# Attention in steps, output products two steps behind, projections spread between score pieces

## The chip, the cores and the metric

The kernel runs on one core of a Trainium2 chip. The metric is the device time in microseconds (us), lower is better. The median of three runs of the kernel before is 2564.09 us, with 2552.84 and 2574.48 as the lowest and highest.

The engines of a core each run their own instruction list in order: TensorE (PE, matmuls; PEld are its weight loads), VectorE (DVE), ScalarE (ACT), GpSimd (POOL) and SyncE (SP, which here mostly issues DMAs). An instruction that waits holds back everything behind it on its engine.

## What is computed

One layer of a streaming encoder: 2048 positions, width 1024, with eight heads of banded attention (a query sees its own 64-frame chunk and eight chunks before it) and four heads of differential attention (each made of two softmax maps over all earlier chunks, the second subtracted with a factor), then an output projection and a gated feed-forward part with a short convolution. Cut to what matters:

```python
h = rmsnorm(x, attn_norm_g[l])
qa, ka, va, qb, kb, vb = jnp.split(h @ w_in[l], 6, axis=-1)
...
# band heads: scores over 9 chunks of 64 keys + relative bias, softmax, times v
# differential heads, per block of 128 queries:
sc = jnp.einsum("bqhd,bkhd->bhqk", qblk, k) * (HEAD_DIM ** -0.5)
sc = jnp.where(allowed, sc + bias, -jnp.inf)
p = jax.nn.softmax(sc, axis=-1).reshape(b, B_HEADS, 2, Q_BLOCK, s)
w = p[:, :, 0] - lam * p[:, :, 1]
o = jnp.einsum("bhqk,bkhe->bqhe", w, v)
...
x = x + jnp.concatenate([oa, ob], axis=-1) @ w_out[l]
u = causal_dwconv(rmsnorm(x, ffn_norm_g[l]) @ w_up[l], conv_w[l], conv_b[l])
gate, val = jnp.split(u, 2, axis=-1)
x = x + (jax.nn.silu(gate) * val) @ w_down[l]
return rmsnorm(x, final_norm_g)
```

## The kernel before

**Numbers.** Every large product is done in float16 with each float32 factor split into a high and a low part; three of the four part products are summed (`TERMS`). So a projection of 512 positions takes 8 x 3 = 24 matmuls of 512 columns, and a block of probabilities times values takes three matmuls.

**Slots.** Attention runs in eight slots, `ORDER = [4, 5, 0, 6, 1, 7, 2, 3]`. Numbers 4 to 7 are the differential heads (long rows: tile i of 128 queries sees 128(i+1) keys, so up to 2048); here they are called B slots, and they are the slots 0, 1, 3 and 5. Numbers 0 to 3 are pairs of band heads (at most 640 keys); these are the A slots 2, 4, 6 and 7. Each slot has 16 tiles of 128 queries, in order, in four groups of four.

**One tile.** Scores go to PSUM for both maps of a piece of up to 512 keys (L426 and L428: the high and the low part of q, into tiles `s`). VectorE adds the bias, takes the running maximum and moves the piece to SBUF in one instruction (L474 in A, L524 in B; `St`). After the last piece ScalarE takes the exponential (L481, L530), in B VectorE combines the two maps (L546), ScalarE and GpSimd split the result into float16 parts `phl` (L482 and L483; L548 and L549), SP issues a DMA that transposes it into `pt` (L484, L551), and TensorE multiplies `pt` with the values into `o` (L495, L557). VectorE takes `o` out (`osb`, L497, L559). Scores, exponential, transpose and output products of one tile are one step of a generator (`attn_a`, `attn_b`).

**Projections.** Beside a slot's attention, the kernel projects what is needed next: q of the following group of 512 positions (`proj_q`, tiles `qs`), and after each group of four tiles k and v of the same positions for the next slot's head (`proj_k`, `proj_v`). Their matmuls are L372, with weights `whl` that `load_w` reads, scales and splits for all three of q, k and v at the start of the slot before. ScalarE and VectorE take each result out of PSUM (`split`, L127 and L128). With two small DMAs for each `qs` tile (L416, L417), issued on ScalarE's queue, q is copied to the other half of the partitions.

**The end of attention.** The output projection (`out_proj`, L625, 768 matmuls of 512 columns, tiles `omm`) is done in two parts. Whole quarters of the first part are put between the tiles of the last slot by the table `LAST`; its weights are loaded and split (`load_wo`) at that slot's start. Then come the feed-forward part's up projection (L762) and down projection (L1161).

**What sets the order.** No order is written out by hand: a scheduler places each instruction in its engine's list, by the order of the code and by priorities. Attention steps run under `high_priority(offset=HA)`, the PSUM evictions of the projections under `HP`; the projection matmuls have no such offset. Buffers that bear on the order: three PSUM banks for projections, four for scores, one for the four small `o` tiles; eight granules of `St`, two `phl`, three `pt`, eight each of `ks` and `vs`, two `qs`, four `whl`, two raw weights.

## Time and profile before

| | us or share |
|---|---|
| median of three runs | 2564.09 (2552.84 to 2574.48) |
| the profiled execution's own time | 2562.97 |
| its span | 2560.9 |
| TensorE busy | 2389.8 (93%) |
| VectorE busy | 1894.7 (74%) |
| ScalarE busy | 1401.5 (55%) |
| GpSimd busy | 1171.0 (46%) |
| mean granted TensorE clock | 0.956 |

Busy time counts instructions that do work. TensorE's matmuls overlap and their ends are modelled, so 100% busy says that something was always under way. The granted clock is TensorE's, as a share of full speed; at a lower clock the same matmuls fill more busy time. A window of the trace gives these figures for a stretch of time, so that stages can be told apart. A wait names the instruction that waited and what released it.

### The profile page before, as it was taken

The numbers are of one execution on the slowest core, as the hardware profiler recorded it, in microseconds if no ns is written. First come the engines' busy times: TensorE is split into PE (matmuls) and PEld (weight loads), VectorE is DVE, ScalarE is ACT, GpSimd is POOL, SyncE is SP. The second block draws the span as 40 slices with busy tenths as digits, with TensorE's granted clock in tenths as the row PEclk, the third lists the DMA queues.
The fourth block names the chain that finished last, engine by engine and source line by source line (L and its number), as shares of the span: only waits on it lengthen the run. The fifth ranks groups of instructions, "written<-read, shape, count | busy, mean of one in ns | idle before, by whom it ended". The sixth has DMA issues, their size and how long they took to land.

```text
span 2560.9 us, 39466 instructions
## 1 busy us (share of the span) xinstructions
PE 2389.8 (93%) x13878; PEld 1146.9 (45%) x13878; DVE 1894.7 (74%) x4391; ACT 1401.5 (55%) x2431; POOL 1171.0 (46%) x1127
## 2 busy tenths in 40 slices
PE   5799998989897999989869999999999999999998
PEld 4544444544454444444434444444444444444443
DVE  6669786877876797757665888888887886656545
ACT  5547556755675567655434656665656564323322
POOL 2315334332433252123343566656665664756654
PEclk8898998989898989989989999999999999999999
DMA  7224545863677359989978333333323329323322
GB/s 211 57 54 88 104 78 103 143 128 73 112 134 137 58 105 200 191 177 255 278 203 207 123 110 116 100 128 104 122 95 126 104 92 404 121 89 110 112 87 78
DMA packets 631222, 340.48 MB, mean 133 GB/s; under 512 B 448920, under 2 KB 597712, under 8 KB 629616
## 3 DMA queue, kind: packets, MB, share of 16 engines
q1 hardware_dynamic: 615264, 316.15, 48.7%
q10 hardware_dynamic: 12592, 10.26, 1.5%
q0 software_dynamic: 3168, 11.56, 1.4%
q8 instruction: 108, 1.77, 0.3%
q14 instruction: 90, 0.74, 0.1%
HBM read 148.87 MB, written 85.21 MB: 91 GB/s over the span
## 4 chain that ended last, share of the span: by engine, by line
PE 53%; DMA 8%; DVE 8%; issue 4%; ACT 4%; POOL 2%; SPq 2%; ACTq 0%; DVEq 0%; POOLq 0%
PE mm L762 27%; PE mm L1161 13%; PE mm L372 7%; DMA pt<-phl 5%; PE omm L625 2%; PE s L428 2%; DMA wd<-gd 2%; PE s L426 1%; SPq L996 1%; PE o L557 1%; DVE St L524 1%; ACT St L481 1%; ACT phl L482 1%; DVE hl L649 1%; DVE St L546 1%
## 5 line engine op out<-in xcount | busy, mean ns | idle before, releaser
L762 PE MATMUL mm<-T,wuhl 128*128 128x512 f16 x3696 | 802.8, 380 | 24.8 <-ACT tmp L933 22.4
L762 PEld LDWEIGHTS <-wuhl 128*128 128x128 f16 x3696 | 361.9, 98 | 457.8 <-issue 25.9
L372 PE MATMUL mm<-h,whl 128*128 128x512 f16 x2208 | 535.1, 389 | 0.1
L1161 PE MATMUL mm<-wd,ghl 128*128 128x512 f16 x1848 | 401.8, 380 | 2.9 <-ACT ghl L127 1.8
L372 PEld LDWEIGHTS <-whl 128*128 128x128 f16 x2208 | 205.7, 100 | 250.1 <-issue 38.2
L549 POOL TENSOR_TENSOR phl<-St,phl 128x1024 f16<-128x1024 f32 (+4 forms) x96 | 155.7, 1632 | 304.2 <-ACT phl L548 292.6
L1161 PEld LDWEIGHTS <-ghl 128*128 128x128 f16 x1848 | 180.7, 98 | 223.4 <-ACT ghl L127 2.9
L961 DVE SCALAR_TENSOR_TENSOR Y<-U,taps,Y 128x1024 f32<-128x1024 f32 x176 | 257.3, 1462 | 3.9 <-ACT Y L957 2.4
L530 ACT ACTIVATE St<-St,nb,sc 128x1024 f32<-128x1024 f32 (+4 forms) x192 | 188.1, 981 | 88.3 <-DVE nb L527 87.5
L426 PE MATMUL s<-ks,qs 128*128 128x128 f16 (+3 forms) x720 | 196.1, 303 | 41.7 <-DVE mxb L524 32.7
L127 ACT ACTIVATE ghl<-wd,gsc 128x384 f16<-128x384 f32 (+1 forms) x176 | 106.6, 659 | 195.6 <-DMA wd<-gd 89.7
L128 DVE SCALAR_TENSOR_TENSOR ghl<-wd,gsc,ghl 128x384 f16<-128x384 f32 (+1 forms) x176 | 136.9, 812 | 95.1 <-ACT ghl L127 94.4
L524 DVE CUSTOM_DVE_ANT_0 St<-s,near,mxb 128x512 f32<-128x512 f32 (+3 forms) x280 | 168.7, 624 | 40.6 <-PE s L428 34.7
L483 POOL TENSOR_TENSOR phl<-St,phl 128x640 f16<-128x640 f32 (+2 forms) x64 | 82.4, 1287 | 243.8 <-ACT phl L482 198.7
L428 PE MATMUL s<-ks,qs 64*128 64x128 f16 (+3 forms) x720 | 182.8, 307 | 0.0
L625 PE MATMUL omm<-wohl,oT 128*128 128x512 f16 x672 | 159.2, 391 | 8.7 <-DVE x L629 8.6
L871 POOL TENSOR_TENSOR Sx<-wuraw 128x512 f32<-128x512 f32 x44 | 77.8, 1769 | 171.5 <-ACT wuraw L862 153.9
L965 ACT ACTIVATE Y<-Y 128x1024 f32<-128x1024 f32 x44 | 46.5, 1057 | 179.7 <-DVE Y L961 179.7
L557 PE MATMUL o<-vs,pt 128*128 128x128 f16 x1632 | 123.9, 231 | 21.0 <-DMA pt<-phl 16.4
L792 DVE SCALAR_TENSOR_TENSOR wdhl<-wdraw,wd_sc,wdhl 128x128 f16<-128x128 f32 x132 | 134.6, 1038 | 11.6 <-ACT wdhl L789 10.9
L428 PEld LDWEIGHTS <-qs 64*128 64x128 f16 x720 | 54.4, 93 | 180.9 <-issue 165.2
L481 ACT ACTIVATE St<-St,nb,sc 128x640 f32<-128x640 f32 (+4 forms) x128 | 107.9, 844 | 39.8 <-DVE nb L478 36.7
(227 smaller groups left out, 3868.6 us busy)
## 6 DMA issues: line engine op xcount, KB each, us to landing
wd<-gd SPq DMA_DIRECT2D x88, 256.0 KB, 2.8
wuraw<-in_w_up_dram SPq DMA_DIRECT2D x42, 512.0 KB, 5.0
gd<-Y SPq DMA_DIRECT2D x42, 512.0 KB, 5.3
wdraw<-in_w_down_dram SPq DMA_DIRECT2D x154, 128.0 KB, 2.8
wd<-wdd SPq DMA_DIRECT2D x11, 1792.0 KB, 12.0
wdd<-wdhl SPq DMA_DIRECT2D x41, 448.0 KB, 2.6
wraw<-in_w_in_dram SPq DMA_DIRECT2D x24, 512.0 KB, 4.3
td<-hl SPq DMA_DIRECT2D x24, 512.0 KB, 4.0
```

The lines of the kernel that those rows point to most:

```text
L128: V.scalar_tensor_tensor(lo, src, scale, hi, ALU.mult, ALU.subtract)
L372: nc.tensor.matmul(ps, lhsT=hl[:, a, c, :], rhs=h[:, b, c, :], start=n == 0, stop=n == 3 * NC - 1)
L426: nc.tensor.matmul(ps[hd], lhsT=qs[:, hd, 0, qc], rhs=ks[:, hd, kc], start=True, stop=False)
L428: nc.tensor.matmul(ps[hd], lhsT=qs[a:b, hd, 1, qc], rhs=ks[a:b, hd, kc], start=False, stop=True)
L524: V.tensor_tensor_reduce(Sm[hd][g][:, a0:a0 + b - a], ps[hd][:, :b - a], bias, 1.0, m[hd], ALU.add, ALU.max, mx[:, hd, f:f + 1])
L530: A.activation(Sm[hd][g], Sm[hd][g], AF.Exp, bias=nb[:, hd:hd + 1], scale=w["sc"], accum_out=l[:, hd, g:g + 1])
L549: nc.gpsimd.tensor_tensor(hl[:, 1], Sm[0][g], hl[:, 0], ALU.subtract)
L557: nc.tensor.matmul(o, lhsT=pt[:, a_, j], rhs=vs[:, c_, kt % 4, :], start=kt == 0 and k_ == 0, stop=kt == i and k_ == 2)
L625: nc.tensor.matmul(ps[n], lhsT=oc[:, a], rhs=wo[ORDER[c]][:, b, n * TG:(n + 1) * TG], start=k == 0, stop=k == 3 * NC - 1)
L762: nc.tensor.matmul(ps, lhsT=hl[:, a, wop, c * P:(c + 1) * P], rhs=Tt[:, b, c, :], start=start and k == 0, stop=k == 11, skip_group_check=n ...
L961: V.scalar_tensor_tensor(Y, self.U[j][:, tap:D + tap], self.u.taps[j][:, tap:tap + 1], Y, ALU.mult, ALU.add)
L1161: nc.tensor.matmul(ps[m].rearrange("p (c n) -> p c n", c=4), lhsT=g[kb][:, a, go], rhs=wd[kb][:, :, c_, wo_], start=kb == k0 and k == 0, s ...
```

## The change

The change rewrites the attention stage's order of work; the feed-forward part and every formula stay.

1. Each tile is cut in two: `front_a`/`front_b` (scores to `pt`) and `back_a`/`back_b` (output products). The back part of a tile is written `LAG = 2` steps after its front.
2. The B slots no longer take the tiles 0 to 15 in order but 0, 15, 1, 14, 2, 13 and so on, a short row beside a long one. Steps run on over slot boundaries.
3. Projections are generators that yield after every 6 matmuls (12 of q). `units(n)` lists what a slot has to project, and each step takes its share (48 chunks over 16 steps; 32 in slot 6, 28 over 11 steps in slot 7), divided over the tile's score pieces.
4. q is projected in halves of 256 positions (tiles `mq` and `qs`, four smaller `qs` buffers), since the tiles are no longer taken in groups of four. That makes 64 such projections of 24 matmuls of 256 columns in place of 32 of 512.
5. The three weights of the next head are scanned and loaded at different steps (`beside`), k of the head after next already at steps 13 and 14. In slot 6 the scans for later stages, and in slot 7 `load_wo`, also have steps of their own.
6. The last slot keeps part of its own k and v projections (groups 2 and 3) as fill; the output projection's first part starts at its step 11, in pulls of four chunks of 6 matmuls.
7. One buffer of `x1k` and the call of `make_profiles` move.

The diff, cut to its core:

```diff
+NH2 = 8
+LAG = 2
...
+        def project(ps, hl, h, t0, t1, step):
             n = 0
             for c in range(NC):
                 for a, b in TERMS:
+                    nc.tensor.matmul(ps, lhsT=hl[:, a, c, :], rhs=h[:, b, c, t0:t1], start=n == 0, stop=n == 3 * NC - 1)
                     n += 1
+                    if n % step == 0 and n < 3 * NC:
+                        yield
...
-            qs = kv.tile([P, 2, 2, TG], F16, name="qs", bufs=2)
-            ps = project(w, tg, 0)
+            ps = ps_mm.tile([P, 2 * P], F32, name="mq", tag="mm")
+            yield from project(ps, w["hl"][0], hT[i0 // 4], i0 % 4 * P, (i0 % 4 + 2) * P, 12)
+            qs = w["q"][w["halves"][k]] = kv.tile([P, 2, 2, 2 * P], F16, name="qs", bufs=4)
...
+        def front_b(w, i):
...
+            for f, (a, b) in enumerate(reversed(pieces(0, W, (F,)))):
+                ps = [ps_s.tile([P, 512], F32, name="s") for hd in range(2)]
+                scores([p_[:, :b - a] for p_ in ps], w, i, a, b)
...
                 yield
...
+        def back_b(w, i):
+            pts, rl = w["P"].pop(i)
...
+            for pt, kt0, n in pts:
+                for j in range(n):
...
+                    if j % 4 == 3 and kt < i:
+                        yield
...
-                    xt = kv.tile([P, D], F32, name="x1k", tag="qs", bufs=2) if pc and sd else \
+                    xt = sb.tile([P, D], F32, name="x1k", tag="HL", bufs=2) if pc and sd else \
...
+                                if k % 6 == 0 and k < 3 * NC:
+                                    yield
...
+            order = list(range(NT)) if p < 4 else [i for a in range(NT // 2) for i in (a, NT - 1 - a)]
...
+        def units(n):
+            w = ws[n]
+            q = [proj_q(w, k) for k in range(2, 8)]
+            if n == NH2 - 1:
+                kv_ = [[proj_k(w, g), proj_v(w, g)] for g in (2, 3)]
+                return q[:2] + kv_[0] + q[2:4] + kv_[1] + q[4:]
+            x = ws[n + 1]
+            k, v = [proj_k(x, g) for g in range(NG)], [proj_v(x, g) for g in range(NG)]
+            qx = [proj_q(x, 0), proj_q(x, 1)]
+            if n == NH2 - 2:
+                return q[:2] + [k[0]] + q[2:4] + [k[1], v[0]] + q[4:] + [v[1]] + qx
+            return q[:2] + k[:2] + q[2:4] + k[2:] + q[4:] + v[:2] + qx + v[2:]
...
+        CHUNKS = {NH2 - 2: 32, NH2 - 1: 28}
+        UNTIL = {NH2 - 1: 11}
...
+                    want = CHUNKS.get(n, 48) * (s_ + 1) // steps - got if s_ < steps else 0
+                    got += want
+                    for k in range(slots):
+                        with tc.high_priority(offset=HA):
+                            next(fr)
...
+                        with tc.high_priority(offset=HA):
+                            pull(back, 2)
+                        pull(fill, want * (k + 1) // slots - want * k // slots)
...
+                    if n == NH2 - 1 and s_ >= steps:
+                        pull([first], 4)
```

How this moves TensorE's list is seen at two places. The first is the long row of tile 14 in slot 5 (head 7). Here `qs_...` is its q, `ks_...` its k, `s_...` the score tiles; `mm_...` is a projection for the next slot with weights `whl_...`. Before, pieces of scores follow one another:

```order
L426 LDWEIGHTS qs_10270
L426 MATMUL s_11032<-ks_9134,qs_10270 128x512
L428 LDWEIGHTS qs_10270
L428 MATMUL s_11032<-ks_9134,qs_10270 128x512
L426 LDWEIGHTS qs_10270
L426 MATMUL s_11033<-ks_9134,qs_10270 128x512
L428 LDWEIGHTS qs_10270
L428 MATMUL s_11033<-ks_9134,qs_10270 128x512
L426 LDWEIGHTS qs_10270
L426 MATMUL s_11040<-ks_8767,qs_10270 128x512
L428 LDWEIGHTS qs_10270
L428 MATMUL s_11040<-ks_8767,qs_10270 128x512
```

In the change, TensorE has at the same tile:

```order
L376 MATMUL mm_10462<-h_568,whl_9896 128x512
L376 LDWEIGHTS whl_9896
L376 MATMUL mm_10462<-h_568,whl_9896 128x512
L438 LDWEIGHTS qs_9948
L438 MATMUL s_10577<-ks_8926,qs_9948 128x512
L440 LDWEIGHTS qs_9948
L440 MATMUL s_10577<-ks_8926,qs_9948 128x512
L376 LDWEIGHTS whl_9896
L376 MATMUL mm_10462<-h_568,whl_9896 128x512
L376 LDWEIGHTS whl_9896
L376 MATMUL mm_10462<-h_568,whl_9896 128x512
L376 LDWEIGHTS whl_9896
```

Projection matmuls of 512 columns now stand before and behind a single piece of scores, where before three pieces' matmuls stand in a row.

The second place is the boundary from slot 4 (A) to slot 5 (B), where the output products of slot 4's last tile are placed (L495 before, L515 after; `pt_...` is a tile's transposed probabilities, `vs_...` its values). Before, the products of the next slot's tiles 0 (`pt_9690`) and 1 (`pt_9721`) follow it directly:

```order
L495 MATMUL o_117<-vs_8082,pt_9431 128x64
L495 LDWEIGHTS pt_9431
L495 MATMUL o_117<-vs_8082,pt_9431 128x64
L557 LDWEIGHTS pt_9690
L557 MATMUL o_117<-vs_8430,pt_9690 128x128
L557 LDWEIGHTS pt_9690
L557 MATMUL o_117<-vs_8430,pt_9690 128x128
L557 LDWEIGHTS pt_9690
L557 MATMUL o_117<-vs_8430,pt_9690 128x128
L557 LDWEIGHTS pt_9721
L557 MATMUL o_117<-vs_8430,pt_9721 128x128
L557 LDWEIGHTS pt_9721
```

In the change, the products of slot 4's last tile (`pt_10097`) stand behind scores of the next slot's first long row (not shown) and a projection of q (`mq_...`, 256 columns):

```order
L376 MATMUL mq_10260<-h_1094,whl_9262 128x256
L376 LDWEIGHTS whl_9262
L376 MATMUL mq_10260<-h_1094,whl_9262 128x256
L376 LDWEIGHTS whl_9262
L376 MATMUL mq_10260<-h_1094,whl_9262 128x256
L515 LDWEIGHTS pt_10097
L515 MATMUL o_117<-vs_8425,pt_10097 128x64
L515 LDWEIGHTS pt_10097
L515 MATMUL o_117<-vs_8425,pt_10097 128x64
L515 LDWEIGHTS pt_10097
L515 MATMUL o_117<-vs_8425,pt_10097 128x64
L515 LDWEIGHTS pt_10097
```

The next slot's own output products (L557 before, L589 after) come only after some 20 more projection matmuls and further scores.

## Rows read from the trace of the kernel before

**Rows 1.** Windows by stage: stretch, length, busy per engine, PEclk, DMA share, GB/s

```profile
core 0: us, PE busy (x) PEld busy (x) DVE busy (x) ACT busy (x) POOL busy (x), PEclk, DMA share, GB/s
...
95.00:263.00 168.00, 151.30 (x900) 70.42 (x897) 126.00 (x396) 93.86 (x183) 63.49 (x36) 0.91 0.38 74
263.00:432.00 169.00, 153.03 (x963) 76.00 (x962) 131.56 (x401) 97.50 (x194) 60.34 (x36) 0.89 0.48 92
432.00:520.00 88.00, 88.00 (x715) 44.61 (x714) 65.49 (x211) 61.65 (x122) 22.87 (x16) 0.97 0.76 135
520.00:698.00 178.00, 159.89 (x1064) 78.85 (x1062) 142.52 (x417) 101.03 (x198) 69.27 (x40) 0.88 0.51 98
698.00:786.00 88.00, 87.94 (x729) 45.34 (x726) 70.04 (x217) 66.25 (x131) 24.04 (x17) 1.00 0.77 144
786.00:959.00 173.00, 150.59 (x1025) 72.35 (x1025) 136.97 (x412) 98.34 (x194) 65.26 (x38) 0.90 0.48 95
959.00:1053.00 94.00, 89.59 (x732) 45.70 (x729) 70.57 (x222) 67.50 (x134) 25.87 (x18) 1.00 0.90 187
1053.00:1315.00 262.00, 240.86 (x1630) 116.44 (x1627) 178.18 (x410) 141.23 (x227) 82.89 (x61) 0.94 0.91 227
1315.00:2561.00 1246.00, 1205.62 (x5593) 547.61 (x5591) 905.93 (x1425) 620.02 (x961) 729.35 (x842) 0.99 0.40 130
```

**Rows 2.** Windows, same columns: the eight gaps of the four long-row slots

```profile
790.00:820.00 30.00, 13.54 (x171) 8.64 (x168) 23.54 (x77) 14.99 (x37) 15.42 (x11) 0.72 0.84 157
920.00:950.00 30.00, 24.05 (x129) 10.11 (x129) 27.68 (x86) 22.37 (x39) 19.86 (x10) 0.72 0.43 96
sum 200.00, PE 134.56 PEld 67.34 DVE 166.73 ACT 116.86 POOL 121.81; mean PE 16.82 PEld 8.42 DVE 20.84 ACT 14.61 POOL 15.23
```

**Rows 3.** Windows, same columns: the stretch between two of these gaps

```profile
828.00:922.00 94.00, 94.00 (x567) 43.17 (x564) 74.57 (x235) 53.86 (x106) 21.81 (x15) 1.00 0.36 69
```

**Rows 4.** Waits of TensorE, 95 to 1053 us: waiting line, releaser, total, times, longest

```profile
PE s L426 <- DVE mxb L524: 32.7, 24, 4.7
PE o L557 <- DMA pt<-phl: 16.4, 5, 8.1
```

**Rows 5.** Waits of TensorE, 1053 to 1315 us

```profile
PE omm L625 <- DVE x L629: 8.6, 3, 6.2
```

**Rows 6.** Timeline of TensorE at two gaps: start, us, instruction [idle before <-releaser]

```profile
815.12 0.82 PE L557 MATMUL o<-vs,pt 128*128 128x128 f16 x6 [8.10 <-DMA pt<-phl]
...
930.87 0.58 PE L426 MATMUL s<-ks,qs 128*128 128x512 f16 x1 [4.73 <-DVE mxb L524]
```

**Rows 7.** Chain of waits, pieces in order of time: start, us, what

```profile
894.08 1.51 PE o L557 x27
...
1423.20 36.28 PE mm L762 x168
```

**Rows 8.** Costliest groups of the page: weight loads of the projections

```profile
L372 PEld LDWEIGHTS <-whl 128*128 128x128 f16 x2208 | 205.7, 100 | 250.1 <-issue 38.2
```

**Rows 9.** Tile qs: count, duration ns min/median/max, first and last start, form

```profile
L127 ACT ACTIVATE qs<-mm x64: 571/592/592, 54.4 to 1104.1; 64x512 f16<-64x512 f32 x64
L128 DVE SCALAR_TENSOR_TENSOR qs<-mm,qs x64: 658/689/695, 56.4 to 1107.0; 64x512 f16<-64x512 f32 x64
L416 ACTq DMA_DIRECT2D qs<-qs x32: 468/468/557, 55.0 to 1101.1; - x32
```

**Rows 10.** Groups by shape, 95 to 1053 us: busy, mean, idle before

```profile
L530 ACT ACTIVATE St<-St,nb,sc 128x1024 f32<-128x1024 f32 x80 | 98.5, 1231 | 57.0 <-DVE nb L527 56.9
...
L546 DVE SCALAR_TENSOR_TENSOR St<-St,ratio 128x1024 f32<-128x1024 f32 x36 | 58.1, 1615 | 0.7
...
L549 POOL TENSOR_TENSOR phl<-St,phl 128x1024 f16<-128x1024 f32 x40 | 87.2, 2183 | 118.4 <-ACT phl L548 110.5 <-issue 7.7
```

**Rows 11.** The transposes of L551: issue ns min/median/max, and landing

```profile
L551 SPq DMA_TRANSPOSE pt<-phl x96: 1168/1648/3821, 101.3 to 982.9; - x96
...
DMA to landing us min/median/max: 2.3/4.2/7.2
```

More of the change, by code (lines that the diff above doesn't have):

```diff
@@ L652, in out_proj, with weights, run @@
                         hl.rearrange("p n a d -> p n (a d)"))
[L653 to L660 removed]
+        def weights(n):
+            p = ORDER[n]
+            order = list(range(NT)) if p < 4 else [i for a in range(NT // 2) for i in (a, NT - 1 - a)]
+            halves = []
+            for i in order:
+                if i // 2 not in halves:
+                    halves.append(i // 2)
+            return dict(p=p, order=order, halves=halves, hl={}, E={}, raw={}, k={}, v={}, q={}, P={}, o={}, ssq={})
+        def run(unit):
+            for _ in unit:
+                pass
+        w = weights(0)
         xts, raws = [], []
@@ L724 @@
-        for _ in out_proj(1):
-            pass
+        run(proj_q(w, 1))
+        make_profiles()
+        ws = [w] + [weights(n) for n in range(1, NH2)]
+        first = out_proj(0)
+        def units(n):
[10 more added lines that the diff above has]
+            return q[:2] + k[:2] + q[2:4] + k[2:] + q[4:] + v[:2] + qx + v[2:]
@@ L728, in down_scale @@
+        attention()
     def down_scale(k1):
```

409 lines of the change are left out of this document (217 added, 192 removed).

## Prediction

> **What bounds the kernel now.** I read the windows by stage first, and there only two columns: TensorE's busy time against the length, and its granted clock. From 1315 us on (feed-forward) TensorE is busy 1205.62 of 1246 us at clock 0.99; the change doesn't touch this half. The three A slots from 432 to 1053 us are the same picture: 88.00 of 88, 87.94 of 88, 89.59 of 94. The four B slots are not: 151.30 of 168, 153.03 of 169, 159.89 of 178 and 150.59 of 173, at clocks of 0.88 to 0.91 [rows 1]. Together they take 688 us, of which TensorE is busy 614.8 and idle 73.2.
>
> Second, windows within the B slots. TensorE's idle time is not spread evenly. Between 828 and 922 us it is busy 94.00 of 94 at clock 1.00 [rows 3], while eight stretches (110 to 130, 230 to 250, 370 to 400, 410 to 430, 530 to 550, 650 to 680, 790 to 820, 920 to 950 us; 200 us in all) hold 200 - 134.56 = 65.4 us of the 73.2. Two of them stand in the rows: TensorE busy 13.54 and 24.05 of 30, clock 0.72 in both [rows 2]. So idle time and low clock come at the same places: a slot's beginning, where the first rows are short, and its last long rows.
>
> Third, the waits. Up to 1053 us TensorE waits mostly for two things: 32.7 us for VectorE to free a score bank and 16.4 us for transposed probabilities [rows 4]. The timeline puts one of each at the two places of the order that are shown with the change: at 815.12 the products of a short row waited 8.10 us for their transpose, with nothing else in the list; at 930.87 a long row's scores waited 4.73 us for VectorE [rows 6]. In both, projections had run out. In the rows between, VectorE works 74.57 of 94 us and is not waited for at all [rows 3]. The B slots thus lose time since the filling is in the wrong places, not because there is too much work for one engine.
>
> **What the B slots' work is worth.** The lost clock is 168 x 0.09 + 169 x 0.11 + 178 x 0.12 + 173 x 0.10 = 72.4 us of full speed [rows 1]. What of it fell into idle time costs nothing: between 72.4 x 0.67 = 49 us (busy as in the gaps, 134.56 of 200) and 72.4 x 0.89 = 65 us (busy as in the whole slots) was lost while busy. The low clock is mostly in the gaps, so I take 50. TensorE's work at full clock is then 614.8 - 50 = 565 us, and 688 - 565 = 123 us is friction. VectorE's work there is 126.00 + 131.56 + 142.52 + 136.97 = 537 us [rows 1], close behind.
>
> **The change, part by part.**
>
> Spreading the projections and alternating short and long rows. A matmul of 512 columns takes 36.28 / 168 = 216 ns at full clock, one of an output product 1.51 / 27 = 56 ns [rows 7]. With these prices I counted the order. Before, the projections beside the eight pairs of steps of slot 3 are worth 2.2, 10.4, 11.4, 13.2, 9.1, 12.3, 5.8 and 9.7 us; after, 8.1, 10.3, 9.8, 9.7, 11.3, 7.0, 9.9 and 5.7. The empty first pair is filled, and the other B slots look alike (slot 5's first pair: 1.3 before, 7.1 after). Over the four B slots projections fall from 290 to 283 us; 7 us move to the last slot. That leaves 558 us of work. The friction lies between nothing left (558) and all 123 left (681). I take 52 left, 610 us or 152 a slot. I don't go lower, for VectorE's share rises to some 90% (below), and the nearest row for that load is the gap at 920, where VectorE is busy 27.68 of 30 and TensorE only 24.05 [rows 2]; I don't go higher, for the loads of a pair of steps after the change are now alike (in slots 3 and 5 TensorE has 15 to 21 us per pair, VectorE 11 to 19), and where filling was there nothing waited [rows 3]. **B slots: 610 - 688 = -78.**
>
> Output products two steps behind. They add no work. Counted in the order, between a long tile's last scores and its first output product TensorE has 20 to 26 us of other work (before: 19 to 30). The chain to be hidden, for two maps of two granules: four exponentials of 1.23, the combination of 1.62, a copy no longer than an exponential, GpSimd's 2.18, an issue of up to 3.82 and a landing of 4.2, together 18 us [rows 10, 11]. It fits, and before, with the same cover, all the long rows gave at most 8 us of waiting (16.4 in five places, 8.10 of it at the short row) [rows 4, 6]. A buffer of `pt` is read out 12 us or more before its third successor's first product at nearly every tile (before: from 7), against 8 for issue and landing. I price it at nothing; if the cover falls short, this is the second rival.
>
> q in halves. 1536 matmuls of 256 columns in place of 768 of 512. Between the 56 ns for 128 columns and 216 for 512 lies 109 ns, so +1.6 us, which is inside the counts above. The evictions go from 64 to 128 on each of ScalarE and VectorE; one of 512 columns takes 0.592 and 0.689 us [rows 9]. The extra lies between 0 (half size, half time) and 64 x 0.689 = 44 us of VectorE; I take 20, ten of them in the B slots: 547 of 610 us, 90%. 64 more DMA issues of 0.468 us on ScalarE's queue [rows 9] are 30 us over eight slots; ScalarE is busy 93.86 to 101.03 us per B slot [rows 1], so the slack covers them.
>
> Weight loads. At each of these matmuls new weights are loaded: 768 more loads of 100 ns each [rows 8]. Output products also load new weights for each, and 27 of them took 1.51 us, less than 27 loads one after the other [rows 7, 8]. I price the loads at nothing.
> The Trainium skill ("TensorE: Matmul & The Clock Gate", Part 3, "What overlaps and what doesn't") says that a weight load overlaps with matmuls under way only when their row groups differ; by it the added loads, all of one row group, would cost 77 us. The row of 27 products contradicts that here.
>
> A slots. TensorE has 265.5 us of work in 270 [rows 1], less 2.6 by the counts. The steps now run over slot boundaries, so B's last long rows reach into them. From 263 (nothing waits) to 284 (8% of friction as in B after); I take 276. **+6.**
>
> Last slot and output projection. Before, TensorE is busy 240.86 of 262 [rows 1]. Projections moved in: 80 matmuls of 512 before, 96 of 512 and 100 of 256 after, 16 x 0.216 + 100 x 0.109 = +14 us. Of the output projection, 278 of 768 matmuls stood before the last scores, now 84: 42 us of TensorE work move behind the attention. If the 21 idle us swallow all, 255 (-7); if the attention is held by VectorE at its old length, +42. Near the middle, **+20**, since VectorE (178.18 of 262) and its waits (8.6 us for `x`) [rows 1, 5] don't hold TensorE for long.
>
> Sum: -78 + 6 + 20 = -52. The profiled execution took 2562.97, so 2511; the median of the runs, 2564.09, is 1.1 above it, which I leave out.
>
> **The rivals.**
>
> *VectorE becomes the bound of the B slots.* Its 547 us run in an in-order list with waits for scores, copies and outputs; if it keeps only 85% busy, B takes 643 us: -45 + 26 = -19, **2544**. For it: it works 83% even over the eight gaps (166.73 of 200) [rows 2]. Against: 92% in the gap at 920.
>
> *Slower: the output products run into their transposes.* Each B slot has eight long rows, 32 in all. A wait of 1.6 us at each eats the 52 us, 2.4 us each makes it slower by 1%. The chain of 18 us would have to become 28 against the 25 of the cover, by POOL, SP and ScalarE serving the short row in between; then 3 us x 32 = 96, **2607**. For it: SP issues in order, and landings reach 7.2 us [rows 11]. Against: the cover before was no longer, and the waits few.
>
> *The added weight loads are not hidden*: 2511 + 77 = **2588**. The row of 27 products speaks against it.
> This is the Trainium skill's rule named above.
>
> *The change fills only the slots' beginnings*, and the long rows' gaps stay: half of the gain in B, -39 + 26 = -13, **2550**. The counts per pair speak against it.
>
> *Better:* friction in B falls to 25 us, A stays, the last slot costs 10: -105 + 10 = -95, **2468**.
>
> **Numbers.** Chances: forecast 0.51 (own range 2480 to 2538), better 0.12, VectorE 0.20, transposes 0.11, weight loads 0.03, beginnings only 0.03. A measurement of this kernel can tell about 1% from no change: faster is below 2538, slower above 2590. Faster: 0.12, nearly all of 0.51 and a quarter of the VectorE case, 0.66; slower: the transposes and a little of the weight loads, 0.12; the rest, 0.22, is the same. The bounds of all terms together reach from 2419 (558, 263, 255) to 2612 (681, 284, 304); 2450 to 2570 leaves out the transposes' case above and a part of the better one below.
>
> **What would show it.** B slots of about 152 us at a clock above 0.95, TensorE without idle stretches at their beginnings; waits for `s` from VectorE under 30 us in all, hardly any for `pt`; A slots near 92; the last slot with the output projection near 282; 256-column matmuls 109 ns apart. VectorE over 90% busy with TensorE idle would mean the first rival, waits of `o` for `pt` at long rows the second, spacing of 200 ns at `mq` the third. If the gaps only move to where the fill now runs out (the last slot's end above all), the forecast is wrong in its first term.

## The result and the profile after

The change takes 2538.15 us (median of four runs, 2536.24 to 2539.51), the kernel before 2564.77 on the same chip (four runs, 2552.84 to 2574.48). The ratio is 0.9898, 95% interval 0.9855 to 0.9940: faster by 27 us, where 52 were forecast. The profiled execution took 2539.1 us (span 2536.9, clock 0.970) against 2562.97 (span 2560.9, clock 0.956).

The windows of the kernel after, cut at its stages (columns as in [rows 1]; the slots in order, then the last slot with the output projection, then the rest):

```profile
core 0: us, PE busy (x) PEld busy (x) DVE busy (x) ACT busy (x) POOL busy (x), PEclk, DMA share, GB/s
93.00:258.00 165.00, 155.90 (x1095) 87.10 (x1092) 129.89 (x384) 96.83 (x195) 59.60 (x33) 0.96 0.44 77
258.00:405.00 147.00, 135.33 (x979) 75.57 (x978) 130.04 (x401) 95.36 (x195) 61.20 (x34) 0.95 0.49 95
405.00:507.00 102.00, 95.03 (x893) 55.73 (x892) 81.31 (x264) 70.19 (x146) 31.22 (x22) 1.00 0.81 144
507.00:660.00 153.00, 145.99 (x1077) 81.09 (x1076) 124.56 (x376) 95.49 (x191) 57.30 (x33) 0.96 0.53 96
660.00:763.00 103.00, 97.66 (x872) 56.11 (x871) 85.55 (x271) 69.58 (x146) 36.50 (x25) 1.00 0.79 145
763.00:911.00 148.00, 139.38 (x1095) 79.36 (x1095) 122.17 (x377) 96.25 (x192) 59.04 (x34) 0.99 0.54 101
911.00:1004.00 93.00, 87.62 (x802) 53.62 (x799) 73.43 (x250) 68.10 (x144) 29.78 (x20) 0.93 0.80 161
1004.00:1263.00 259.00, 245.58 (x1692) 123.03 (x1691) 175.06 (x409) 131.69 (x214) 63.08 (x48) 0.97 0.99 238
1263.00:2537.00 1274.00, 1214.48 (x5590) 549.13 (x5588) 900.51 (x1442) 634.14 (x984) 744.76 (x855) 0.98 0.40 128
```

The B slots (165, 147, 153 and 148 us) are now busy 94% of their length at clocks of 0.95 to 0.99, where [rows 1] show 89% at 0.88 to 0.91. The A slots (102, 103, 93) are longer than before. The last part, 1274 us, is longer too. Cut by first scores and the last product of the output projection, the stages compare so:

| us | before | after | difference | forecast |
|---|---|---|---|---|
| ahead of attention | 95.1 | 93.0 | -2 | 0 |
| four B slots | 687.5 | 613.6 | -74 | -78 |
| three A slots | 271.3 | 297.2 | +26 | +6 |
| last slot to the last product of `out_proj` | 262.1 | 259.5 | -3 | +20 |
| from there to the end | 1244.9 | 1273.5 | +29 | 0 |

Since steps now run over slot boundaries, work moves between B and A; the robust figure is the attention stretch of the seven slots, from the first score to the first score of the last slot: 958.8 to 910.8, -48 (forecast -72). The rest gives 26 of it back (forecast +20). TensorE's waits in that stretch (waiting line, releaser, total, times, longest):

```profile
PE s L438 <- DVE mxb L543: 22.6, 29, 2.6
PE s L438 <- DVE mx L484: 10.8, 13, 1.5
PE o L515 <- DMA pt<-phl: 3.9, 2, 2.6
PE o L589 <- DMA pt<-phl: 3.5, 4, 1.6
```

The first and the fourth line are of B, the others of A. The waits for score banks (`s`) are 22.6 us in B and 10.8 in A; before they were 32.7 in B [rows 4] and 3.3 in A. Those for transposes are 7.4 us in all, where B alone had 16.4 [rows 4] and A 5.9.

Where the last part loses its 29 us is seen at its start. Timeline of TensorE, then ScalarE, then SyncE, of the kernel after (start, us, instruction, [idle before <-releaser]):

```profile
1262.56 0.81 PE L660 MATMUL omm<-wohl,ost_l 128*128 128x512 f16 x3
1286.27 1.03 PE L865 MATMUL mm<-T,wuhl 128*128 128x512 f16 x2 [22.90 <-ACT wuhl L985]
1292.34 4.07 PE L865 MATMUL mm<-T,wuhl 128*128 128x512 f16 x10 [5.04 <-POOL wuhl L983]
...
1268.91 1.13 ACT L675 ACTIVATE xn<-x1k,r 128x1024 f32<-128x1024 f32 x1
...
1285.15 1.06 ACT L985 ACTIVATE wuhl<-wuraw 128x1024 f16<-128x1024 f32 x1
...
1271.34 1.21 SPq L941 DMA_DIRECT2D wuraw<-in_w_up_dram  x2
```

The output projection ends at 1263.4, and the next product waits 22.90 us for the weights `wuhl`. In the kernel before the up projection runs on at once, and a wait comes later:

```profile
1315.20 0.81 PE L625 MATMUL omm<-wohl,ost_l 128*128 128x512 f16 x3
1315.85 10.52 PE L762 MATMUL mm<-T,wuhl 128*128 128x512 f16 x48
1348.79 35.19 PE L762 MATMUL mm<-T,wuhl 128*128 128x512 f16 x156 [22.42 <-ACT tmp L933]
```

Over the 72 and 78 us from the end of `out_proj` on, TensorE is idle 43.7 us after and 24.0 before, +20; the other 9 us are longer busy time (1214.1 against 1204.6 over the whole part; the clock is 0.70 in those 72 us and 0.87 in the 78).

The cause suspected: item 7 moves `x1k` into the buffers `HL`, which in the program's allocation (156128 to 165344 of a partition) lie under the first `wuhl` (154080 to 168416); before, it lay in q's old buffers (121216 to 129408). `x1k` is last read in the ScalarE row at 1268.91; the raw weights `wuraw` of the first `wuhl` are fetched at 1271.34 (before: at 1224.09), and `wuhl` is first written at 1285.15.

### The profile page after: what moved, and what is told of

It is laid out like the page before. It is cut to its first block, busy times and chain, and to the rows that moved or that the text cites. A ratio compares the mean times of both kernels' runs of the same rounds, so it can differ in the third digit from the quotient of the medians.

```text
span 2536.9 us, 41286 instructions
## 1 busy us (share of the span) xinstructions
PE 2377.2 (94%) x14646; PEld 1209.7 (48%) x14646; DVE 1890.7 (75%) x4455; ACT 1411.6 (56%) x2495; POOL 1170.2 (46%) x1127
## 4 chain that ended last, share of the span: by engine, by line
PE 48%; DMA 2%; POOL 2%; issue 1%; DVE 1%; ACT 1%; SPq 0%; ACTq 0%; DVEq 0%; POOLq 0%
PE mm L865 30%; PE mm L1264 13%; PE omm L660 5%; DMA wd<-gd 2%; SPq L1099 0%; POOL wuhl L983 0%; DMA wdraw<-in_w_down_dram 0%; DMA pt<-phl 0%; POOL Sx L974 0%; POOL wd L1241 0%; ACT wuraw L965 0%; DMA T<-td 0%; POOL wd L1242 0%; POOL wd L1244 0%; POOL wd L1243 0%
## 5 line engine op out<-in xcount | busy, mean ns | idle before, releaser
L865 PE MATMUL mm<-T,wuhl 128*128 128x512 f16 x3696 | 812.0, 382 | 43.8 <-ACT wuhl L985 28.4
L376 PEld LDWEIGHTS <-whl 128*128 128x128 f16 x2976 | 274.8, 100 | 205.9 <-issue 36.6
L376 PE MATMUL mm<-h,whl 128*128 128x512 f16 x1440 | 354.4, 389 | 2.9 <-DVE qs L130 2.5
L569 POOL TENSOR_TENSOR phl<-St,phl 128x1024 f16<-128x1024 f32 (+7 forms) x96 | 157.6, 1652 | 229.1 <-ACT phl L568 169.6
L438 PE MATMUL s<-ks,qs 128*128 128x128 f16 (+3 forms) x720 | 194.4, 297 | 42.9 <-DVE mxb L543 22.6
L376 PE MATMUL mq<-h,whl 128*128 128x256 f16 x1536 | 202.2, 278 | 3.9 <-DVE qs L130 3.4
L660 PE MATMUL omm<-wohl,oT 128*128 128x512 f16 x672 | 154.0, 382 | 1.4 <-DVE wohl L130 1.4
L895 DVE SCALAR_TENSOR_TENSOR wdhl<-wdraw,wd_sc,wdhl 128x128 f16<-128x128 f32 x132 | 128.8, 996 | 14.2 <-ACT wdhl L892 13.8
```

The lines of the kernel that those rows point to most:

```text
L376: nc.tensor.matmul(ps, lhsT=hl[:, a, c, :], rhs=h[:, b, c, t0:t1], start=n == 0, stop=n == 3 * NC - 1)
L438: nc.tensor.matmul(ps[hd], lhsT=qs[:, hd, 0, qc], rhs=ks[:, hd, kc], start=True, stop=False)
L569: nc.gpsimd.tensor_tensor(hl[:, 1], Sm[0][g], hl[:, 0], ALU.subtract)
L660: nc.tensor.matmul(ps[n], lhsT=oc[:, a], rhs=wo[ORDER[c]][:, b, n * TG:(n + 1) * TG], start=k == 0, stop=k == 3 * NC - 1)
L865: nc.tensor.matmul(ps, lhsT=hl[:, a, wop, c * P:(c + 1) * P], rhs=Tt[:, b, c, :], start=start and k == 0, stop=k == 11, skip_group_check=n ...
L895: V.scalar_tensor_tensor(dst, src, scale, h, ALU.mult, ALU.subtract)
```

## The experiments

Ratios are to the kernel before on the same chip, with 95% intervals; "A+B" is the attention stretch (958.8 before, 910.8 after). It is read from one execution of each kernel, and the four of the kernel before alone lie 22 us apart, so differences of a few us in it are not read.

### Where x1k lies

The change with `x1k` elsewhere, and the kernel before with it in `HL`:

```diff
-                    xt = sb.tile([P, D], F32, name="x1k", tag="HL", bufs=2) if pc and sd else \
+                    xt = granule("x1k") if pc and sd else \
```

> The change with one edit: x1k, the row buffer that the change moved from the kv pool to the phl buffers (tag HL), takes a granule (tag S) instead. Theory A: the first split weights of the up projection (wuhl) lie over the phl buffers in SBUF, so in the change they cannot be written before the output projection has read its last x1k; away from there the up projection starts right behind the output projection. After the change TensorE idled 43.8 us between 1263 and 1335 us, before 24.8 us between 1316 and 1394; the stretch from the last output-projection product to the end was 28.6 us longer. A expects 19 to 28 us less, 2510 to 2519 us. Theory B: ScalarE and GpSimd need that time for the weights wherever x1k lies, and the earlier end of attention only uncovers it: 2533 to 2543 us.

```diff
-                    xt = kv.tile([P, D], F32, name="x1k", tag="qs", bufs=2) if pc and sd else \
+                    xt = sb.tile([P, D], F32, name="x1k", tag="HL", bufs=2) if pc and sd else \
```

> The kernel before with this one edit of the change alone: x1k under tag HL in place of the qs buffers. A: the first split of wuhl, at 1244 us before, moves behind the last read of x1k near 1310 us, and the time rises by 15 to 30 us to 2580 to 2595 us. B: no difference, 2555 to 2575 us.

Measured 0.9902 (0.9873 to 0.9930; 2542.25 us) and 1.0034 (1.0021 to 1.0046; 2578.43 us). Windows of the last slot and of the rest, first of the change with `x1k` in a granule:

```profile
999.60:1282.70 283.10, 247.92 (x1694) 123.09 (x1693) 189.12 (x427) 145.37 (x237) 80.65 (x61) 0.96 0.93 220
1282.70:2534.30 1251.60, 1210.77 (x5588) 548.85 (x5587) 899.13 (x1425) 620.75 (x961) 727.68 (x842) 0.99 0.41 130
```

and of the kernel before with `x1k` in `HL`:

```profile
1057.10:1305.30 248.20, 234.72 (x1610) 114.19 (x1606) 165.29 (x391) 128.14 (x204) 64.56 (x48) 0.97 0.95 236
1305.30:2577.70 1272.40, 1211.73 (x5589) 548.36 (x5588) 916.52 (x1442) 633.30 (x984) 744.81 (x855) 0.98 0.40 128
```

The place is confirmed in both directions: 1273.5 falls to 1251.6, and 1244.9 rises to 1272.4. But the last slot moves the other way (259.5 to 283.1; 262.1 to 248.2). So the late start by itself costs about 9 us in the kernel before, and moving `x1k` out of `HL` gains nothing in the change: its output projection ends later by as much. Why early weights lengthen the last slot, no run separates.

How the place acts is seen in the first fetch of `wuraw`. With `x1k` in `HL`, SyncE issues it 1.3 us after the last read of `x1k` has ended (1271.34 after 1270.04), and in the kernel before with `x1k` in `HL` 0.6 us after it (1312.84 after 1312.28); with `x1k` elsewhere it is issued 92 us ahead of the end of the output projection (the kernel before) and 148 us ahead (the granule). At 1271.34 no wait is recorded: the fetch stands late in SyncE's list. The row sums and the scaling of the weights then take until 1285.15.

### The longer A slots

In the A slots after, TensorE is busy 279.6 us (before, cut alike, 266.8) and idle 17.7 (4.5). Of the 13 us of added busy time 9 to 11 are scores, by two ways of sharing out overlapping matmuls. The timeline of the kernel before shows two orders of the same four score matmuls of 256 columns, high part with 128 weight rows and low part with 64, for two maps:

```profile
840.64 0.39 PE L426 MATMUL s<-ks,qs 128*128 128x256 f16 x2
840.96 0.28 PE L428 MATMUL s<-ks,qs 64*128 64x256 f16 x2
841.18 4.49 PE L372 MATMUL mm<-h,whl 128*128 128x512 f16 x20
...
922.46 0.28 PE L426 MATMUL s<-ks,qs 128*128 128x256 f16 x1
922.67 0.28 PE L428 MATMUL s<-ks,qs 64*128 64x256 f16 x1
922.89 0.28 PE L426 MATMUL s<-ks,qs 128*128 128x256 f16 x1
923.10 0.28 PE L428 MATMUL s<-ks,qs 64*128 64x256 f16 x1
923.32 0.23 PE L426 MATMUL s<-ks,qs 128*128 128x128 f16 x1
```

Grouped (both 128-row, then both 64-row), four take 841.18 - 840.64 = 0.54 us; alternating, 923.32 - 922.46 = 0.86. The granted clock is 1.00 at both places. In the A slots, low-part products that stand side by side fell from 76 pairs to 49, of 117 possible. Two ways to group them: both maps in one two-bank tile,

```diff
...
-                ps = [ps_s.tile([P, 512], F32, name="s") for hd in range(2)]
+                pb = ps_s.tile([P, 2, 512], F32, name="s", bufs=2)
+                ps = [pb[:, hd] for hd in range(2)]
...
```

> The change with the two maps' score tiles in one PSUM tile of two banks (two such tiles in place of four of one bank), so that the two products with the high part of q and the two with the low part can stand next to each other; counted in the order, low-part products standing next to each other rise from 138 to 357 pairs, and changes between weights of 128 and of 64 rows fall from 1164 to 726. Theory C: such a change costs about 0.1 us (a score product of 128 columns took 0.152 us ahead of one and 0.057 or 0.067 without), and the second of two neighbouring low-part products costs nothing (0.003 us to the next start); then 438 x 0.1 = 44 us and some 20 us of products fall away where TensorE sets the pace: 2485 to 2515 us. Rival D: TensorE must now wait until VectorE has read both maps, with only two tiles in flight; waits for VectorE take back all of it: 2535 to 2570 us.

the same with `x1k` in a granule,

> Both edits on the change: x1k in a granule and the two maps in one PSUM tile. They act in different stages (the start of the feed-forward part, the attention), so A and C add: 2460 to 2495 us; with A alone true 2510 to 2545 us, with C alone 2485 to 2515 us.

and a dependency that orders two instructions of TensorE without a semaphore wait (the edge), which puts the first map's low part behind the second map's high part,

```diff
...
+                lo = nc.tensor.matmul(ps[hd], lhsT=qs[a:b, hd, 1, qc], rhs=ks[a:b, hd, kc], start=False, stop=True)
+                if hd == 0:
+                    tc.add_manual_dep(lo.ins, hi[1].ins.name, ... NoSync ...)
```

> The change with one ordering edge on TensorE in each group of four score products: the low-part product of the first map comes behind the high-part product of the second; the four PSUM banks stay single. In the order, neighbouring low-part products rise from 138 to 346 pairs, changes between weights of 128 and 64 rows fall from 1164 to 748. Theory C (the split pairs cost what the A slots lost beside the forecast): 416 x 0.1 us = 42 us of TensorE work and up to 20 us of hidden products, all of it gained in the A slots where TensorE sets the pace (with paired banks their busy time fell by 10 us a slot), about half in the B slots: 2498 to 2520 us. Rival D: VectorE gets the first map's scores later, and what TensorE saves is waited for: 2533 to 2545 us.

and that in the A slots alone (`hd == 0 and w["p"] < 4`):

> The same edge in the A slots alone (217 neighbouring pairs, 1006 changes of rows). C: the three A slots lose the 11 us by which their scores had become dearer, and some more, and the fourth a little: 2515 to 2528 us. D: 2533 to 2543 us.

The two-bank tile took 0.9965 (0.9951 to 0.9979; 2560.67 us): slot 2 is busy 85.5 us instead of 95.1, slot 4 87.6 instead of 97.3, but banks now come free only in pairs: the waits for `s` rise from 33.4 to 58.8 us, and B from 613.6 to 644.7. The edit also pairs the tiles of the transposes ahead of attention, and that part takes 100.4 us instead of 93.0. With the granule it is 0.9998 (0.9985 to 1.0011; 2568.51). The edge gave 0.9838 (0.9809 to 0.9866; 2532.40) and, in A alone, 0.9821 (0.9801 to 0.9840; 2525.63). Slot 2 with the edge:

```profile
409.00:501.70 92.70, 84.80 (x864) 51.85 (x863) 76.79 (x259) 68.79 (x142) 32.56 (x23) 0.98 0.84 150
```

84.80 us busy of 92.70, against 95.1 of 102.1. Yet with the edge in A alone the three A slots are busy 266.5 us, back at the level of before, and take 298.3 (297.2 in the change): idle time went from 17.7 to 31.9, and the waits for A's score banks, which VectorE frees, from 10.8 to 24.1. So the order of scores is what made TensorE's work in A longer, but it isn't what sets the length of A. With the edge everywhere the A slots take 281.6 us, but B 620.3, so A+B falls by 9 us only (901.9). The profiled execution with the edge in A alone is 14 us below that of the change; these come from the last slot (259.5 to 251.7), which is an A slot and has the edge too, and from the rest (1273.5 to 1268.8), which the edit doesn't touch. With the edge everywhere those two take 261.5 and 1274.3, so I don't claim them for the edge.

### Alternation, spreading, lag

The forecast's main term rested on these three. Tiles in order:

```diff
-            order = list(range(NT)) if p < 4 else [i for a in range(NT // 2) for i in (a, NT - 1 - a)]
+            order = list(range(NT))
```

> The change with the B slots' tiles in order 0 to 15; spread, lag and halves stay. Theory E: the alternation is what evens out the two engines' load in the B slots; without it VectorE's long rows come together again at a slot's end and half of the 74 us that the B slots gained goes: 2565 to 2580 us. Rival F: the spread of the projections and the lag do it; 2533 to 2548 us.

Projections pulled only at every fourth step:

```diff
-                    want = CHUNKS.get(n, 48) * (s_ + 1) // steps - got if s_ < steps else 0
+                    want = CHUNKS.get(n, 48) * (s_ + 1) // steps - got if s_ < steps and (s_ % 4 == 3 or s_ == steps - 1) else 0
```

> The change with the projections handed out only at every fourth step (all that four steps would have got, divided over that step's pieces); order of tiles and lag stay. Theory G: the spread is worth much; between the bunches TensorE has only scores and output products, and waits for VectorE as before: 2560 to 2585 us. Rival H: the scheduler pulls the projections to where TensorE is free in any case: 2533 to 2545 us.

`LAG = 0` (the back part right behind its front):

> The change with each tile's output products written right behind its own front, as before (lag 0); alternation and spread stay. Theory I: most of the 48 us gained in the A and B slots goes, since output products wait again for their transposes and hold up what stands behind them: 2565 to 2590 us. Rival J: the scheduler places them late in any case, as soon as there is filling: 2533 to 2548 us.

Then one alone: lag without the other two, spreading without the other two, and none of the three.

> The change with the B slots' tiles in order and the projections handed out at every fourth step, both at once; the lag of two steps stays. Neither cost anything alone. Theory I: the lag is what gains in the attention, and the scheduler finds the rest itself: 2533 to 2548 us against 2538 of the change. Rival K: order and spread stand in for each other, and without both TensorE runs dry as before: 2555 to 2575 us.

> The change with lag 0 and the B slots' tiles in order: of the three only the spread of the projections is left (with the halves of q and the weights loaded at steps of their own). Theory I: 2565 to 2590 us. Rival J: 2533 to 2550 us. Were the spread worth much by itself, it would show here against the next run.

> The change with lag 0, tiles in order and projections at every fourth step: what is left of the change is q in halves, the weights loaded at steps of their own, the k of the head after next ahead of time, projections without a fixed place behind each group, and the last slot's new order. Theory I (or K): about the time of the kernel before, 2560 to 2590 us. Rival J: 2535 to 2550 us, and then the gain lies in what is left.

| | ratio | us | A+B |
|---|---|---|---|
| the change | 0.9898 (0.9855 to 0.9940) | 2538.15 | 910.8 |
| in order | 0.9884 (0.9863 to 0.9906) | 2542.15 | 904.9 |
| bunched | 0.9857 (0.9836 to 0.9879) | 2535.49 | 900.9 |
| no lag | 0.9861 (0.9833 to 0.9888) | 2534.57 | 920.4 |
| lag only | 0.9835 (0.9803 to 0.9867) | 2529.05 | 905.1 |
| spreading only | 0.9839 (0.9810 to 0.9867) | 2529.20 | 899.5 |
| none of them | 0.9898 (0.9871 to 0.9925) | 2544.28 | 907.2 |

Without any of the three the kernel keeps the whole gain. Lag or spreading alone may be worth 0.6%, with intervals that hardly touch those of the change; all three together are worth nothing. The explanation of the prediction fell with this. A variant with the lag alone and the edge in A showed that these don't add up: 0.9836 (0.9809 to 0.9863; 2527.93).

> The change with tiles in order, projections at every fourth step, and the ordering edge on the scores of the A slots. If the two edits (ratios 0.9835 and 0.9821 of before, where the change has 0.9898) add: 0.976, some 2505 us. If the second only takes up what the first has already: 0.982, 2520 us.

### The weights of the next head

What was left is item 5, which the prediction hadn't priced. In the change, k's weights loaded late, at the slot's first steps:

```diff
...
+                todo[0, 0] = lambda: scan_w(x, ORDER[n + 1], 1)
+                todo[0, 1] = lambda: load_w(x, 1)
...
-                todo[13, 0] = lambda: scan_w(ws[n + 2], ORDER[n + 2], 1)
-                todo[14, 1] = lambda: load_w(ws[n + 2], 1)
```

> The change with the weights of the next head's k scanned and loaded at the slot's first step instead of at steps 13 and 14 of the slot before. Theory L: projections at the slot's beginning are what the kernel before lacked, and they are there only since these weights are; without, the beginnings run dry again: 2560 to 2585 us. Rival M: the scheduler shifts q's projections and others into the beginnings: 2533 to 2548 us.

All three scanned and loaded at the slot's first step, as before the change:

```diff
...
+                def now():
+                    for j in (1, 2, 0):
+                        scan_w(x, ORDER[n + 1], j)
+                        load_w(x, j)
+                    load_bias(x, ORDER[n + 1])
+                todo[0, 0] = now
```

> The change with all three weights of the next head scanned and loaded at the slot's first step, as before the change. L: 2560 to 2590 us, at most 10 us above the run before it. Rival N: it is the loads' bunching on ScalarE and GpSimd, at the slot's beginning, that costs: this run 2560 to 2590 us, the run before it 2533 to 2548 us. M: both 2533 to 2548 us.

The kernel before with k's weights loaded a slot ahead:

```diff
...
+                if tg == 3 and n < 6:
+                    pre = weights()
+                    load_w(pre, ORDER[n + 2], 1)
```

> The kernel before with one edit: the weights of k for the head after next are loaded at the slot's last group of tiles instead of at the next slot's start. L: most of the 48 us is gained by this alone: 2515 to 2540 us on the 2565 of before. M or N: 2555 to 2575 us (N: perhaps 10 us less).

Late k: 0.9868 (0.9841 to 0.9895; 2534.74), A+B 905.5: no loss. All at the start: 1.0007 (0.9994 to 1.0020; 2573.45), A+B 947.5: the whole gain gone. By slots this can't be read, since work moves between them: the four B slots take 611.4 us there, as in the change, and the three A slots 336.1 instead of 297.2. The kernel before with k ahead: 0.9948 (0.9932 to 0.9964; 2555.17), A+B 948.1, so k alone is worth some 11 of the 48 us.

What happens at a slot's start is in the kernel before's trace. SyncE's and GpSimd's, ScalarE's and TensorE's rows at the start of slot 5:

```profile
810.25 0.57 SPq L316 DMA_DIRECT2D wraw<-in_w_in_dram  x1
...
806.26 2.12 POOL L333 TENSOR_TENSOR whl<-wraw,whl 128x1024 f16<-128x1024 f32 x1 [2.12 <-ACT whl L332]
...
814.60 1.15 ACT L140 ACTIVATE whl<-wraw,gam 128x1024 f32<-128x1024 f32 x1 [4.90 <-DMA wraw<-in_w_in_dram]
...
815.89 0.59 PE L146 MATMUL am<-ws_ss,ones 128*128 128x1 f32 x2
816.34 6.04 PE L372 MATMUL mm<-h,whl 128*128 128x512 f16 x21
```

There are two raw buffers for three weights, and the first two weights hold them. GpSimd's first split (806.26) releases one; the third fetch follows at 810.25, ScalarE scans it at 814.60 after 4.90 us of waiting for it to land, TensorE forms the row sums `am` at 815.89, and at 816.34 runs the first projection since 789. That is the current head's own q (its result goes into `qs` at 823.57), whose weights had been split by 689; in TensorE's list it stands behind the products that wait for a transpose [rows 6] and behind the `am` of the third weight, whose code comes ahead of it. The waits for `am` themselves are 9.1 us in the whole stretch of the kernel before; in the experiment with all three at the start they are 24.3 us (3 times, up to 11.1).

So the last two experiments separate item 5 from everything else. The kernel before, with nothing but the weights taken apart, k's a slot ahead (v scanned after the third tile of the first group and loaded after the fourth, q at tiles 7 and 8, k of the head after next at 13 and 14):

```diff
+        def scan_w(p, j, raw=None):
...
+            return raw, hl, ss
...
-                for j in (1, 2, 0):
-                    load_w(nw, ORDER[n + 1], j)
...
+                        attend(tiles, 3)
+                        nw["raw"][j] = scan_w(ORDER[n + 1], j)
+                        attend(tiles, 1)
+                        load_w(nw, ORDER[n + 1], j)
...
+                        attend(tiles, 1)
+                        pre["raw"][1] = scan_w(ORDER[n + 2], 1)
+                        attend(tiles, 1)
+                        load_w(pre, ORDER[n + 2], 1)
```

> The kernel before with the three weights of the next head scanned and loaded at steps of their own, as in the change: v at the tiles 3 and 4, q at 7 and 8, k of the head after next at 13 and 14; all else as before (tiles in order, output products with their tile, q whole, projections behind groups of four, old last slot). Theory N (weights apart are the gain): 2515 to 2540 us on 2568 of before. Rival O: they are a part only, no more than k a slot ahead gave (0.9948): 2550 to 2568 us, and the rest of the gain needs q in halves or projections without a fixed place.

And the change with all three early again, but each scanned a step ahead of its load, so that `am` finds its input ready:

```diff
...
+                todo[0, 0] = lambda: (scan_w(x, ORDER[n + 1], 1), scan_w(x, ORDER[n + 1], 2))
+                todo[1, 0] = lambda: (load_w(x, 1), load_w(x, 2), scan_w(x, ORDER[n + 1], 0))
+                todo[2, 0] = lambda: (load_w(x, 0), load_bias(x, ORDER[n + 1]))
```

> The change with all three weights at the slot's start, but scanned a step before they are loaded (k and v scanned at step 0, loaded at 1; q scanned at 1, loaded at 2). If all at the start (1.0007) cost time by holding TensorE at their row sums: 2533 to 2550 us. If by taking up GpSimd and ScalarE: 2558 to 2575 us.

The first took 0.9809 (0.9788 to 0.9831; 2521.97 us), the lowest ratio of all kernels here, though some other intervals overlap it. Its slot 5 starts with projections under way (timeline of TensorE), and the first 30 us of that slot stand against the same 30 us of the kernel before (windows):

```profile
753.63 4.27 PE L376 MATMUL mm<-h,whl 128*128 128x512 f16 x19
...
778.56 4.70 PE L376 MATMUL mm<-h,whl 128*128 128x512 f16 x21
...
753.00:783.00 30.00, 29.14 (x251) 15.32 (x249) 18.50 (x71) 17.69 (x39) 7.92 (x6) 1.00 0.83 141
...
785.00:815.00 30.00, 13.65 (x221) 9.57 (x219) 23.48 (x73) 16.56 (x39) 13.62 (x9) 0.78 0.78 150
```

29.14 of 30 us busy at full clock, against 13.65 at 0.78; ScalarE has the same work (17.69, 16.56), GpSimd 7.92 instead of 13.62. The attention stretch in windows of the kernel before, the change, none of the three, all weights at the start, and the weights apart alone:

```profile
95.10:1053.90 958.80, 881.14 (x6132) 433.86 (x6129) 743.08 (x2272) 586.08 (x1150) 331.14 (x199) 0.92 0.56 109
...
93.00:1003.90 910.90, 856.81 (x6803) 488.52 (x6800) 746.84 (x2318) 591.70 (x1205) 334.65 (x199) 0.97 0.60 111
...
93.80:1001.00 907.20, 840.31 (x6782) 484.96 (x6779) 727.95 (x2318) 590.38 (x1203) 327.19 (x199) 0.96 0.60 113
...
95.40:1042.90 947.50, 865.53 (x6813) 495.81 (x6811) 741.23 (x2334) 593.13 (x1210) 331.56 (x200) 0.93 0.57 111
...
96.10:1009.00 912.90, 860.53 (x6121) 425.69 (x6118) 742.65 (x2272) 586.39 (x1155) 324.25 (x199) 0.96 0.59 114
```

912.9 us with the weights apart alone, so 46 of the change's 48 us. Of these 46, 25 are idle time of TensorE (77.7 to 52.4 us) and 21 are shorter busy time for the same matmuls (881.14 to 860.53), at a granted clock of 0.96 instead of 0.92.

That the slots' beginnings are the place shows in the first 30 us from each of the seven slots' first scores. The sums of these seven windows, for the kernel before, the change, none of the three, all weights at the start, the weights apart alone, and the second experiment:

```profile
sum 210.00, PE 166.76 PEld 95.09 DVE 141.79 ACT 136.24 POOL 75.66; mean PE 23.82 PEld 13.58 DVE 20.26 ACT 19.46 POOL 10.81
...
sum 210.00, PE 207.03 PEld 119.33 DVE 158.83 ACT 129.25 POOL 62.04; mean PE 29.58 PEld 17.05 DVE 22.69 ACT 18.46 POOL 8.86
...
sum 210.00, PE 199.90 PEld 124.44 DVE 146.36 ACT 135.43 POOL 81.06; mean PE 28.56 PEld 17.78 DVE 20.91 ACT 19.35 POOL 11.58
...
sum 210.00, PE 157.09 PEld 89.00 DVE 164.20 ACT 128.59 POOL 106.28; mean PE 22.44 PEld 12.71 DVE 23.46 ACT 18.37 POOL 15.18
...
sum 210.00, PE 202.52 PEld 113.45 DVE 136.07 ACT 134.60 POOL 78.31; mean PE 28.93 PEld 16.21 DVE 19.44 ACT 19.23 POOL 11.19
...
sum 210.00, PE 171.22 PEld 93.09 DVE 171.32 ACT 126.61 POOL 95.96; mean PE 24.46 PEld 13.30 DVE 24.47 ACT 18.09 POOL 13.71
```

TensorE is idle there for 43, 3, 10, 53, 7 and 39 us of 210. The beginnings are empty where the weights are prepared together and filled where they are taken apart, with or without the three parts of the order.

The second took 0.9954 (0.9936 to 0.9972; 2558.70): TensorE waits only 4.8 us for `am`, but A+B is 933.0, so three fifths of the loss stays ((933.0 - 910.8) / (947.5 - 910.8)). The wait for `am` is thus the smaller part of the loss; the larger one comes with the weights being prepared in one lump. Whether ScalarE's and GpSimd's time for it or the later place of the projections in TensorE's list costs that, no run separates.

## Why the prediction was right and wrong

**B slots, -78: the size was right (-74), the cause was not.** The step that failed is "In both, projections had run out", and with it the sentence that filling was in the wrong places and that alternating and spreading would mend it. That the beginnings lacked filling was right (43 us idle there before, 3 after); that projections had run out was not. At 815 the current head's q projection could have run, but stood behind a row sum of weights that were fetched at 810.25 only. The prediction read this gap by the instruction that ended it, the product that waited 8.10 us for a transpose "with nothing else in the list" [rows 6]. Its part on the change leaves out item 5, the one that is worth 46 us alone. The count of projections per pair of steps explains nothing of the gain: with none of the three the stretch is 907.2. The other place that the prediction named, the long rows at a slot's end, didn't get better: outside the beginnings TensorE was idle for 34 us of the stretch before and is for 51 after. So -74 against -78 is luck, and over the stretch as a whole it was -48 against -72. VectorE, forecast at 90% of B, works 506.66 of 613 us (129.89 + 130.04 + 124.56 + 122.17), 83%, and doesn't bound it: TensorE is busy 94%.

**A slots, +6: measured +26, mis-sized.** This is the term that made the time miss most, 20 us. Two things were left out. Scores were priced by their count, though their order costs 0.54 or 0.86 us for four, 9 to 11 us in all; and waits for score banks came up here (10.8 us, before 3.3). The experiment with the edge shows that the second binds: with the work back at 266.5 us A is as long, and these waits are 24.1. The forecast of less than 30 us of waits for `s` failed by them (33.4).

**Last slot +20, the rest 0: measured -3 and +29.** Their sum, +26, is near the 20, but the split was wrong: "the change doesn't touch this half" overlooked item 7, by which the fetch of the next stage's first weights comes after this stage's last read of `x1k`. The last part has a wait of 22.90 us at its start by that. With `x1k` in a granule the two are 283.1 and 1251.6, so +21 and +7: the forecast's split, and the same sum.

**Lag, 0: right.** Waits for `pt` fell to 7.4 us in all; the slower rival didn't occur. **q in halves: right in the spacing, too dear in the evictions.** Timeline of TensorE and the two eviction groups (count, ns min/median/max):

```profile
103.12 5.40 PE L376 MATMUL mq<-h,whl 128*128 128x256 f16 x48
...
L129 ACT ACTIVATE qs<-mq x128: 359/378/378, 54.3 to 1074.3; 64x256 f16<-64x256 f32 x128
L130 DVE SCALAR_TENSOR_TENSOR qs<-mq,qs x128: 393/422/429, 55.8 to 1076.7; 64x256 f16<-64x256 f32 x128
```

48 matmuls of 256 columns in 5.40 us, the last one 0.28: (5.40 - 0.28) / 47 = 109 ns, as worked out, and the added weight loads are hidden. The evictions cost 128 x 0.378 - 64 x 0.592 = +10.5 us of ScalarE and 128 x 0.422 - 64 x 0.689 = +9.9 of VectorE, where 20 were taken for VectorE and none for ScalarE.

So of the sum -52, A and the last two stages together came out 26 us dearer (52 against 26), and B's term 4 short, with 2 us gained ahead of it: -74 + 52 - 2 = -24 in the spans. The range, 2450 to 2570, held the time; the likeliest case's own range, up to 2538, ended just at it.

## What to carry to other kernels

When an engine idles while other work for it is ready, look in its list for what stands ahead of that work, and follow that instruction back to its fetch; preparing the next stage's weights one at a time, well ahead, with the scan a step before the load, was worth 2% here (0.9809), more than the whole change that contains it (0.9898). Before believing that an order written out by hand is what helped, take each part of it away, and then all: the kernel without any of the three was as fast here. When a buffer moves, look which buffer of the next stage will lie on the same bytes.

## What the runs showed of the hardware

The order of products with 128 and with 64 weight rows has a price. Two neighbouring 64-row products, which lie in different halves of the rows, start 0.003 us apart (median of 143 pairs in the kernel before). A 256-column product with 128 rows is followed after 0.109 us by the next one with 128 rows and after 0.205 us by one with 64; from 64 to 128 rows it is 0.212 us (medians of the kernel after). So each change costs about 0.1 us, and that is the 0.54 against 0.86 us above. The weight load (0.09 to 0.10 us) starts 0.004 us ahead of its product at such a change, so it is not hidden there. The Trainium skill ("TensorE: Matmul & The Clock Gate", Part 3, "The mechanism") says that tiles of different row groups run at the same time; the 0.003 us agree with it.

Weight loads between products of the same 128 rows are hidden: 256-column matmuls follow each other at 109 ns with a new load of some 100 ns [rows 8] for each. The Trainium skill ("TensorE: Matmul & The Clock Gate", Part 3, "What overlaps and what doesn't") lets a load overlap only when its row group differs from that of the matmul under way; by it they would be some 200 ns apart, an estimate from 109 + 100. The trace decides against it here.
